# Strassen weight sums made by adding transfers from GpSimd

## The chip, the cores and the metric

One core of a Trainium2 chip runs the whole program in one launch. The metric is the device time of an execution in microseconds (us); the median of three runs is given. The engines are TensorE (PE; its weight loads are shown as PEld), VectorE (DVE), ScalarE (ACT), GpSimd (POOL) and SyncE (SP), which here issues nearly all loads. All work on SBUF, with matmul results in PSUM, and 16 DMA engines move data between device memory and SBUF.

## What is computed

A decoder trunk of two layers over 512 tokens with 16 meta tokens ahead of them, width 1024. Each layer is an FFN, a mixer (gated linear attention in the first layer, windowed attention in the second) and another FFN, each between two RMS norms:

```python
def swiglu(x, w_in, w_out):
    gate, up = jnp.split(x @ w_in, 2, axis=-1)
    return (jax.nn.silu(gate) * up) @ w_out

for layer in range(DEPTH):                      # DEPTH = 2, D_FF = 2816 = 22 tiles of 128
    g = norm_gains[layer]
    h = h + 0.5 * rmsnorm(swiglu(rmsnorm(h, g[0]), w_ffn_in[layer, 0], w_ffn_out[layer, 0]), g[1])
    hn = rmsnorm(h, g[2])
    mix = ...                                   # gla_mixer, or swa_mixer over shared k, v
    h = h + rmsnorm(mix, g[3])
    h = h + 0.5 * rmsnorm(swiglu(rmsnorm(h, g[4]), w_ffn_in[layer, 1], w_ffn_out[layer, 1]), g[5])
```

The four FFNs are where the change lies.

## The kernel before

All is in float32; a product is made of three fast matmuls, for which each operand is split in a high part and a rest. A weight tile comes from device memory into a *raw* tile of 128 x 512 (a pool of `RAWS` tiles, reused in turn). ScalarE copies it, rounded, into the first half of a `w` tile, and VectorE writes raw minus that copy into the second half: that is a *split*. Then TensorE may use the `w` tile, and the raw tile is free for a later load.

Each FFN goes over its 22 hidden tiles in chunks of 4, 6, 6 and 6. The first chunk is computed plainly. In each of the other three, a hidden tile needs a gate weight g and an up weight u, each 128 x 1024; they are taken together as a 2 x 2 block matrix with the blocks 11 and 12 (the halves of g) and 21 and 22 (the halves of u), and multiplied with the tokens by a Strassen scheme: seven products instead of eight, of twelve matmuls each. Their weight operands are 11, 12, 22 and the four sums

- s1 = 21 + 22, s3 = 11 + 21, s2 = s1 + 11, s4 = s2 + 12.

With four FFNs and 18 such hidden tiles in each there are 72 pairs, and twelve chunks of six pairs, which are called stages here. A stage ends with the output projection of its six hidden tiles (names `y` and `Y`).

The order of TensorE's instructions is written down while the program is built, by a small planner (class `Flow`): it advances a clock by the estimated time of each matmul, and coroutines that split, evacuate and prefetch are put in where their time has come. `load_unit` issues the loads of the next weight unit, `split_pair` (L251) splits the seven operands of a pair at steps of `STEP`, `slot` holds a split back until one of the `w` tiles may be taken, and `prefetch` asks for units up to a number of slots ahead, with at most `CHAINS` = 2 pairs unfinished. SP carries the loads, in order; a load waits only until the raw tile that it reuses has been split. `Strassen.head`, `body` and `tail` give the products in the order 11, then s4 and 22 of the pair before, then s1, s2, 12, s3. Between them ScalarE copies banks away (`d` at L909, `c` at L915 and L917) and VectorE sums (`c` at L922, L931, L937, L938), so that a bank can be used again.

In `split_pair`, the sums are made by VectorE in place in the four raw tiles (L266), between the splits. GpSimd makes square sums for the norms (L447) and roots; it issues no transfers.

Of the kernel before, what the change touches and what calls it, by code (L numbers as in the profile page):

```python
# [13 lines left out]
ALU = mybir.AluOpType  # L14
# [15 lines left out]
L1 = [(16, 256), (272, 256)]  # L30
L1W = [(16, 512)]
SLOTS = 32
RAWS = 8
RING = 10
STEP = 1.1
CHAINS = 2
# [103 lines left out]
def trunk_kernel(ctx: ExitStack, tc, a, out, last_out):  # L140
    nc = tc.nc
    pe, act, dve, pool, sp = nc.tensor, nc.scalar, nc.vector, nc.gpsimd, nc.sync
    flow = Flow()

    cp = ctx.enter_context(tc.tile_pool(name="cp", bufs=1))
    rp = ctx.enter_context(tc.tile_pool(name="rp", bufs=RAWS))
    hp = ctx.enter_context(tc.tile_pool(name="hp", bufs=SLOTS))
# [14 lines left out]
    def pair_tile(name, dt=F32R):  # L162
        return hp.tile([P, 2, TOK], dt, tag="pair", name=name)
# [54 lines left out]
    used, asked, freed, ahead, cap, dma_end = [0], [0], [0], [16], [len(units)], [0.0]  # L218
# [10 lines left out]
    def slot(i):  # L229

        while live[0] + sum(n for j, n in owed.items() if j < i) >= limit[0]:
            yield room[0]
        live[0] += 1
        owed[i] -= 1

    def raw_tile(name):
        return rp.tile([P, 512], F32, tag="raw", name=name)
# [7 lines left out]
    def split_unit(i, raws):  # L245
        yield 2.2
        for raw, m in raws:
            yield from slot(i)
            split_part(i, raw, m)

    def split_pair(i, raws):  # L251


        r11, r12, r21, r22 = raws
        parts, ready = loaded[i]

        def part(name, src):
            yield from slot(i)
            w = pair_tile(f"w{i}_{name}")
            act.activation(w[:, 0, :512], src, AF.Copy)  # L260
            dve.tensor_tensor(w[:, 1, :512], src, w[:, 0, :512].bitcast(F32), op=ALU.subtract)  # L261
            parts[name].append(w)
            ready[name].finish(flow)

        def add(dst, src):
            dve.tensor_tensor(dst, dst, src, op=ALU.add)  # L266

        yield 2.2
        yield from part("11", r11)
        add(r11, r21)  # L270
        add(r21, r22)
        yield STEP
        yield from part("s1", r21)
        yield STEP
        yield from part("s3", r11)
        add(r11, r22)
        yield STEP
        yield from part("s2", r11)
        yield STEP
        yield from part("12", r12)  # L280
        add(r12, r11)
        yield STEP
        yield from part("s4", r12)
        yield STEP
        yield from part("22", r22)
        chains[0] -= 1
        prefetch()

    def load_unit():
        i = len(loaded)  # L290
        asked[0] += costs[i]
        owed[i] = costs[i]
        if isinstance(units[i], list):
            g, u = units[i]
            chains[0] += 1
            raws = [raw_tile(f"raw{i}_{k}") for k in range(4)]
            for k in (2, 0, 1, 3):
                sp.dma_start(raws[k], (g, u)[k // 2][:, k % 2 * 512 : (k % 2 + 1) * 512])
                dma_end[0] = max(dma_end[0], flow.clock) + 512 * 1.5e-3
            names = ("11", "12", "22", "s1", "s2", "s3", "s4")  # L300
            loaded.append(({k: [] for k in names}, {k: Job(None) for k in names}))
            gen = split_pair(i, raws)
        else:
            n = units[i].shape[-1]
            raws = []
            for c in range(0, n, 512):
                m = min(512, n - c)
                raws.append((raw_tile(f"raw{i}_{c}"), m))
                sp.dma_start(raws[-1][0][:, :m], units[i][:, c : c + m])
            dma_end[0] = max(dma_end[0], flow.clock) + n * 1.5e-3  # L310
            loaded.append([])
            gen = split_unit(i, raws)
        split_jobs.append(flow.spawn(gen, dma_end[0] - flow.clock))

    def prefetch():
        while len(loaded) < cap[0] and asked[0] + costs[len(loaded)] <= freed[0] + ahead[0]:
            if isinstance(units[len(loaded)], list) and chains[0] == CHAINS:
                break
            load_unit()
# [1149 lines left out]
    raws = [[raw_tile(f"raw{i}_{c}") for c in (0, 512)] for i in range(2)]  # L1469
# [18 lines left out]
    x.rjob[0] = flow.spawn(factors(0, opened), SQUARES)  # L1488
    dma_end[0] = 1.0
    load_unit()  # L1490
    load_unit()
    load_h(1, 0, 2, 4, 6)
    flow.spawn(second(), SECOND)
# [134 lines left out]
```

## Time and profile before

| what | value |
|---|---|
| time, median of 3 runs | 1878.98 us (1878.68 to 1879.55) |
| span of the profiled execution | 1876.7 us |
| its distance to the median | 2.3 us; no separate time of the profiled execution is listed |
| instructions in the span | 37,247 |
| mean GB/s of all DMA | 93 |
| bytes through SP's queue | 171.74 MB |

The page gives busy times by engine, and the span in 40 slices; a group of instructions is listed by its line, engine, operation and tiles, with its count, total and mean time, and behind the bar the idle time of its engine just before it and what ended that idle time. A matmul's time there is longer than the step to the next one, since matmuls overlap. The chain of waits goes back from the last instruction, at each step to what released it.

### The profile page before, as it was taken

How to read it: one execution, taken by the hardware profiler on the slowest of the kernel's cores; microseconds unless marked ns; L12 is line 12 of the kernel's file. 1: busy time of each engine (PE TensorE's matmuls, PEld its weight loads, DVE VectorE, ACT ScalarE, POOL GpSimd, SP SyncE). 2: the span in 40 equal slices, each digit the busy share in tenths (PEclk: the TensorE clock that was granted, in tenths of full speed). 3: DMA queues.
4: the chain of work that ended last, by engine and by line, in shares of the span. 5: the costliest groups of instructions: out<-in, count | busy, mean ns of one | idle time of the engine just before them, and what ended most of it. 6: DMA issues, size and time to landing. Idle time of an engine off the chain costs nothing.

```text
span 1876.7 us, 37247 instructions
## 1 busy us (share of the span) xinstructions
PE 1866.2 (99%) x14463; PEld 1784.7 (95%) x14463; DVE 1395.9 (74%) x2837; ACT 1027.2 (55%) x2309; POOL 163.6 (9%) x295
## 2 busy tenths in 40 slices
PE   9999999999999999999999999999999999999998
PEld 9999999999999999999999898989988898989898
DVE  7885858767564788585887886868777679858585
ACT  5663535654446566363674553535767856636364
POOL 2000000330001300000033000000320140000002
PEclk9999999999999999999999999999999999999999
DMA  5333333421123123233351223233421212333331
GB/s 172 98 96 101 93 106 96 138 69 57 62 63 113 46 91 102 91 102 96 102 175 46 69 88 115 89 114 95 143 74 52 69 46 74 101 104 103 102 114 59
DMA packets 102273, 174.70 MB, mean 93 GB/s; under 512 B 11856, under 2 KB 24016, under 8 KB 102096
## 3 DMA queue, kind: packets, MB, share of 16 engines
q1 hardware_dynamic: 101664, 171.74, 29.3%
q8 instruction: 113, 1.85, 0.4%
q14 instruction: 64, 0.52, 0.1%
q10 hardware_dynamic: 432, 0.59, 0.1%
HBM read 169.66 MB, written 2.10 MB: 92 GB/s over the span
## 4 chain that ended last, share of the span: by engine, by line
PE 90%; DVE 7%; ACT 2%; issue 1%; DMA 0%; POOL 0%; DVEq 0%; SPq 0%; ACTq 0%; POOLq 0%
PE y L177 31%; PE a L177 19%; PE x L177 19%; PE c L177 8%; PE d L177 5%; PE o L177 1%; DVE raw L266 1%; ACT w_s L260 1%; DVE w_s L261 1%; PE e L177 1%; DVE w L261 1%; PE po L177 1%; DVE w L242 1%; PE sa L177 1%; PE pt L189 1%
## 5 line engine op out<-in xcount | busy, mean ns | idle before, releaser
L261 DVE TENSOR_TENSOR w_s<-raw,w_s 128x512 fp32r<-128x512 f32 x288 | 193.8, 690 | 130.1 <-ACT w_s L260 128.3
L177 PE MATMUL y<-hidl0f,w 128*128 128x256 f32 (+1 forms) x2112 | 262.4, 285 | 1.1 <-DVE hidl0f L453 0.9
L177 PEld LDWEIGHTS y<-hidl0f,w 128*128 128x128 f32 x2112 | 259.3, 188 | 2.2 <-DVE hidl0f L453 1.5
L242 DVE TENSOR_TENSOR w<-raw,w 128x512 fp32r<-128x512 f32 x376 | 235.4, 654 | 32.1 <-ACT w L241 30.3
L260 ACT ACTIVATE w_s<-raw 128x512 fp32r<-128x512 f32 x288 | 175.3, 628 | 150.8 <-DVE raw L266 137.6
L177 PE MATMUL y<-hidl1f,w 128*128 128x512 f32 (+1 forms) x1344 | 251.4, 346 | 0.8 <-DVE hidl1f L453 0.4
L177 PEld LDWEIGHTS y<-hidl1f,w 128*128 128x128 f32 x1344 | 212.2, 188 | 36.0 <-DVE hidl1f L942 1.6
L241 ACT ACTIVATE w<-raw 128x512 fp32r<-128x512 f32 x376 | 206.9, 586 | 41.9 <-PE y L177 29.9
L266 DVE TENSOR_TENSOR raw<-raw,raw 128x512 f32<-128x512 f32 x288 | 197.9, 687 | 5.5
L447 POOL TENSOR_TENSOR acc_post<-acc_post,sq_post 128x256 f32<-128x256 f32 (+1 forms) x77 | 62.6, 813 | 1534.0 <-ACT sq_post L446 1531.6
L261 DVE TENSOR_TENSOR w<-raw,w 128x512 fp32r<-128x512 f32 x216 | 148.3, 687 | 29.8 <-ACT w L260 29.0
L260 ACT ACTIVATE w<-raw 128x512 fp32r<-128x512 f32 x216 | 134.0, 621 | 41.6 <-PE y L177 41.0
L177 PE MATMUL x<-x_l0m,w 128*128 128x272 f32 (+1 forms) x1152 | 152.0, 288 | 0.0
L177 PEld LDWEIGHTS x<-x_l0m,w 128*128 128x128 f32 x1152 | 143.3, 188 | 2.7 <-issue 1.7
L706 DVE TENSOR_TENSOR Y<-y,Y 128x256 f32<-128x256 f32 (+2 forms) x175 | 81.8, 473 | 72.1 <-PE y L177 71.5
L177 PE MATMUL a<-zl0f_t,w_s 128*128 128x264 f32 x864 | 117.2, 285 | 0.0
L177 PE MATMUL a<-zl1f_t,w_s 128*128 128x256 f32 x864 | 114.7, 282 | 1.0 <-ACT c L917 0.5
L177 PEld LDWEIGHTS a<-zl1f_t,w_s 128*128 128x128 f32 x864 | 107.4, 188 | 3.0 <-ACT c L917 2.0
L177 PEld LDWEIGHTS a<-zl0f_t,w_s 128*128 128x128 f32 x864 | 109.9, 188 | 0.3
L177 PE MATMUL x<-x_l0f,w 128*128 128x256 f32 (+1 forms) x768 | 97.7, 287 | 1.2 <-ACT w L241 0.8
L177 PEld LDWEIGHTS x<-x_l0f,w 128*128 128x128 f32 x768 | 94.7, 188 | 2.2 <-ACT w L241 1.0
L177 PE MATMUL x<-x_l1f,w 128*128 128x256 f32 (+1 forms) x576 | 93.1, 320 | 0.5 <-ACT x_l1f L475 0.5
(513 smaller groups left out, 3216.6 us busy)
## 6 DMA issues: line engine op xcount, KB each, us to landing
raw<-in_w_in SPq DMA_DIRECT2D x352, 256.0 KB, 2.9
raw<-in_w_out SPq DMA_DIRECT2D x96, 256.0 KB, 3.2
raw<-in_w_last SPq DMA_DIRECT2D x48, 256.0 KB, 3.1
raw<-in_gla_in SPq DMA_DIRECT2D x48, 256.0 KB, 3.2
raw<-in_w_out SPq DMA_DIRECT2D x64, 128.0 KB, 2.9
raw<-in_gla_out SPq DMA_DIRECT2D x16, 256.0 KB, 2.8
raw<-in_w_q SPq DMA_DIRECT2D x16, 256.0 KB, 4.5
raw<-in_swa_out SPq DMA_DIRECT2D x16, 256.0 KB, 2.8
```

What stands on the lines that cost most here:

```text
L177: inst = pe.matmul(o, lhs, rhs, start=start, stop=stop, skip_group_check=onto)
L189: pe.transpose(o, src, ident)
L241: act.activation(w[:, 0, :m], raw[:, :m], AF.Copy)
L242: dve.tensor_tensor(w[:, 1, :m], raw[:, :m], w[:, 0, :m].bitcast(F32), op=ALU.subtract)
L260: act.activation(w[:, 0, :512], src, AF.Copy)
L261: dve.tensor_tensor(w[:, 1, :512], src, w[:, 0, :512].bitcast(F32), op=ALU.subtract)
L266: dve.tensor_tensor(dst, dst, src, op=ALU.add)
L447: pool.tensor_tensor(sums[0][:, :n], sums[0][:, :n], t[:, :n], op=ALU.add)
L706: dve.tensor_tensor(y, p[:, :n], y, op=ALU.add)
```

## The change

The four sums are no longer made by VectorE. Each pair now takes seven raw tiles: 11, 12 and 22 as before, and one tile for each sum. SP loads one addend of each sum into its tile by a plain transfer (21 into s1 and into s3, 11 into s2, 12 into s4). GpSimd then issues four transfers that add their source to what the tile holds: 22 from device memory to s1, 11 from device memory to s3, the finished s1 to s2, and the finished s2 to s4, the last two from SBUF to SBUF. The splits run in the order 11, s1, s2, 12, s3, s4, 22. The pool of raw tiles grows from 8 to 14, and the scratch space reserved in SBUF for such transfers goes from the default to 4096 bytes per partition. The planner's figure for the end of a pair's transfers counts 11 of them instead of 4.

```diff
-RAWS = 8
+RAWS = 14
...
-        r11, r12, r21, r22 = raws
+        r11, r12, r22, s1, s3, s2, s4 = raws
...
-        def add(dst, src):
-            dve.tensor_tensor(dst, dst, src, op=ALU.add)
-
         yield 2.2
         yield from part("11", r11)
-        add(r11, r21)
-        add(r21, r22)
         yield STEP
-        yield from part("s1", r21)
+        yield from part("s1", s1)
         yield STEP
-        yield from part("s3", r11)
-        add(r11, r22)
-        yield STEP
-        yield from part("s2", r11)
+        yield from part("s2", s2)
         yield STEP
         yield from part("12", r12)
-        add(r12, r11)
         yield STEP
-        yield from part("s4", r12)
+        yield from part("s3", s3)
+        yield STEP
+        yield from part("s4", s4)
         yield STEP
         yield from part("22", r22)
...
-            raws = [raw_tile(f"raw{i}_{k}") for k in range(4)]
-            for k in (2, 0, 1, 3):
-                sp.dma_start(raws[k], (g, u)[k // 2][:, k % 2 * 512 : (k % 2 + 1) * 512])
-                dma_end[0] = max(dma_end[0], flow.clock) + 512 * 1.5e-3
+            a11, a12, a21, a22 = (b[:, c : c + 512] for b in (g, u) for c in (0, 512))
+            r11, r12, r22, s1, s3, s2, s4 = raws = [raw_tile(f"raw{i}_{k}") for k in range(7)]
+            for r, src in ((s1, a21), (s3, a21), (s2, a11), (r11, a11), (s4, a12), (r12, a12), (r22, a22)):
+                sp.dma_start(r, src)
+            for r, src in ((s1, a22), (s3, a11), (s2, s1), (s4, s2)):
+                pool.dma_start(r, src, accum_op=ALU.add)
+            dma_end[0] = max(dma_end[0], flow.clock) + 11 * 512 * 1.5e-3
...
-    nc = bacc.Bacc("TRN2", target_bir_lowering=False, num_devices=1)
+    nc = bacc.Bacc("TRN2", target_bir_lowering=False, num_devices=1, dynamic_dma_scratch_size=4096)
```

## The prediction

> **What bounds the kernel now.** I read the page's shares first, then the chain that ended last, then the stages by windows, then who waits for whom, and last the single products of one stage.
>
> ```profile
> PE 1866.2 (99%) x14463; PEld 1784.7 (95%) x14463; DVE 1395.9 (74%) x2837; ACT 1027.2 (55%) x2309; POOL 163.6 (9%) x295
> ...
> PE 90%; DVE 7%; ACT 2%; issue 1%; DMA 0%; POOL 0%; DVEq 0%; SPq 0%; ACTq 0%; POOLq 0%
> ...
> L266 DVE TENSOR_TENSOR raw<-raw,raw 128x512 f32<-128x512 f32 x288 | 197.9, 687 | 5.5
> ```
>
> TensorE is busy for all but 10.5 us of the span of 1876.7 us. The third row is the work that the change takes away: 288 VectorE adds, four for each of 72 weight pairs, 687 ns each. They look like a large prize (197.9 us, and the chain goes through VectorE for 7%), so the question is whether TensorE ever waits for them. The Strassen stages answer it (one row per stage; columns are busy us and counts, then clock, DMA share and GB/s):
>
> ```profile
> 180.00:243.00 63.00, 63.00 (x519) 63.00 (x518) 50.17 (x92) 36.90 (x79) 0.00 (x0) 1.00 0.35 102
> 277.00:340.00 63.00, 63.00 (x516) 62.84 (x515) 51.05 (x91) 38.55 (x81) 0.00 (x0) 1.00 0.36 113
> 883.00:946.00 63.00, 63.00 (x517) 62.85 (x516) 50.94 (x91) 38.49 (x80) 0.00 (x0) 1.00 0.37 112
> 1585.00:1648.00 63.00, 62.12 (x507) 60.84 (x506) 54.70 (x99) 37.50 (x83) 0.00 (x0) 1.00 0.35 109
> ```
>
> In the first three TensorE (63.00 of 63.00) has no gap, with VectorE at 80%; the fourth, the first such stage of the last FFN, is the worst of the twelve and loses 0.9 us. TensorE's own waits say the same (the first rows; the longest five come to 3.7 us, and those that end on ACT's copies `c` and `d`, which may stand behind a wait for the adds, to 0.9):
>
> ```profile
> PE busy L1443 <- DVE eps L1495: 1.0, 1, 1.0
> PE y L177 <- DVE hidl0f L453: 0.9, 3, 0.3
> PE x L177 <- ACT w L241: 0.8, 1, 0.8
> PE a L177 <- ACT c L917: 0.5, 1, 0.5
> PE x L177 <- ACT x_l1f L475: 0.5, 1, 0.5
> PE a L177 <- ACT d L909: 0.4, 1, 0.4
> ```
>
> So TensorE sets the time, its clock is 1.00 in these stages, and its instructions stand in the same order in the built changed program (13,981 before and after, none moved). What the change can give is bounded by the gaps; what it can cost is not.
>
> **What is removed.** Four adds per pair, 4 x 0.687 = 2.75 us of VectorE out of the 10.27 us that a pair takes, and with them ACT's wait for them:
>
> ```profile
> ACT w_s L260 <- DVE raw L266: 137.6, 164, 2.7
> ```
>
> These 137.6 us are ACT idling off the chain: TensorE is gapless over the stages in which they lie. Worth on the path: the 0.9 us of waits above that end on ACT inside the stages, and part of the 0.9 us for `hidl0f` where the factors of the first pair are made beside the first splits. I take 1.5 us, between 0 and the 10.5 us that TensorE idles at all; it lies near the low end because most of those 10.5 us are at the start, the end and in the mixers, where no pair is split.
>
> **What is added: transfers.** Per pair, SP issues 7 plain loads in place of 4, and GpSimd 4 adding transfers.
>
> ```profile
> 5.00:20.00 15.00, 13.85 (x106) 13.14 (x105) 13.59 (x22) 13.89 (x35) 6.08 (x7) 1.00 1.05 375
> raw<-in_w_in SPq DMA_DIRECT2D x352, 256.0 KB, 2.9
> L298 SPq DMA_DIRECT2D raw<-in_w_in x288: 327/328/1541, 56.0 to 1806.4; - x144
> DMA to landing us min/median/max: 2.2/3.0/6.6
> ```
>
> The first row is the opening, the one stretch where the 16 DMA engines are full (share 1.05): 375 GB/s, so 262,144 bytes take 0.70 us of all engines. Seven loads are 4.9 us. An adding transfer has to bring in both its source and its destination; its engine time is bounded by 0.70 us (one pass) and, if reads set the pace, 1.40 us (two passes). I take 1.40, since both operands pass: 4.9 + 5.6 = 10.5 us per pair, against 10.27 us of TensorE; by one pass it would be 7.7. [...] Full engines are still not a full stage: a stage of six pairs and its output projection repeats every 97 us (first two rows of the stages), and needs 6 x 10.5 + 8 x 1.5 x 0.70 = 71 us of DMA, 74%. SP's issuing is 7 x 0.328 = 2.3 us per pair, hidden in SP's own waits for free raw tiles.
>
> **What is added: waits in a row on GpSimd.** The built order on its queue is, for each pair, s1, s3, s2, s4. s2 adds the finished s1 to its tile, s4 adds the finished s2, and the next pair's s1 stands behind s4. Call L the time from GpSimd's start on an adding transfer to its landing, and i its own time for one. In steady state GpSimd needs per pair: L (s1 lands), L (s2 lands), i (s4 sent): P = 2L + i. For i the nearest row is a GpSimd instruction on a tile of similar size:
>
> ```profile
> L447 POOL TENSOR_TENSOR acc_post<-acc_post,sq_post 128x256 f32<-128x256 f32 (+1 forms) x77 | 62.6, 813 | 1534.0 <-ACT sq_post L446 1531.6
> ```
>
> I take i = 0.8 us. L is a plain landing (3.0 median) + a second pass (0.70) + i = 4.5 us; its bounds are 2.2 (the fastest plain landing) and 13.2 (two of the slowest, 6.6). So P = 2 x 4.5 + 0.8 = 9.8 us, under 10.27: GpSimd keeps up, by 0.5 us. [...]
>
> **How late may a sum be?** One pair in products of 12 matmuls (start, length):
>
> ```profile
> 197.05 1.62 PE L177 MATMUL a<-zl0f,w 128*128 128x264 f32 x12
> 198.50 1.62 PE L177 MATMUL c<-zl0f,w_s 128*128 128x264 f32 x12
> 199.96 1.64 PE L177 MATMUL a<-zl0f_t,w 128*128 128x264 f32 x12
> 201.43 1.64 PE L177 MATMUL c<-zl0f_t,w_s 128*128 128x264 f32 x12
> 202.91 1.63 PE L177 MATMUL a<-zl0f_t,w_s 128*128 128x264 f32 x12
> 204.38 1.64 PE L177 MATMUL d<-zl0f,w 128*128 128x264 f32 x12
> 205.85 1.63 PE L177 MATMUL a<-zl0f_t,w_s 128*128 128x264 f32 x12
> 207.32 1.61 PE L177 MATMUL a<-zl0f,w 128*128 128x264 f32 x12
> ...
> 197.95 0.42 DVE L922 TENSOR_TENSOR c<-a,c 128x264 f32<-128x264 f32 x1
> 204.58 0.39 ACT L917 ACTIVATE c<-a 128x264 f32<-128x264 f32 x1
> ...
> L261 DVE TENSOR_TENSOR w_s<-raw,w_s 128x512 fp32r<-128x512 f32 x288 | 193.8, 690 | 130.1 <-ACT w_s L260 128.3
> L260 ACT ACTIVATE w_s<-raw 128x512 fp32r<-128x512 f32 x288 | 175.3, 628 | 150.8 <-DVE raw L266 137.6
> ```
>
> The first eight are 11 of pair m, s4 and 22 of m-1, then s1, s2, 12, s3 of m, and 11 of m+1: a pair every 10.27 us, a product every 1.47; below them stand the sum `v` (0.42), a copy of a bank (0.39) and the two halves of a split (0.69 and 0.63). Put t = 0 at the end of s1 (202.9). In the changed order, s3 of pair m is split just before t = 0, which frees its raw tile, and then SP sends s3, s2 and the rest for pair m+2, since 14 raw tiles are two pairs. They land at 3.3; GpSimd sends s3 and then s2 at about 4.3, and s2 lands at 4.3 + L = 8.8. ACT comes to the split of that s2 after the copy of s2 of m+1, at 11.75 + 0.4 + 0.6 = 12.7. Behind it on ACT stand the copies for the next products, and on VectorE the sum `v` that must be out of bank `a` before 22 of m+1 starts at 17.6; with 0.7 + 0.7 + 0.4 us of VectorE and 0.6 of ACT in between, ACT may start that split as late as 15.2 with no harm. Slack: 15.2 - 4.3 - L = 10.9 - L, here 6.4 us. At the start of a stage the splits of its first pair run early, under the output projection, so the first three pairs' sums are there, and only the last three of six live on the chain. The chain hurts where two steps of drift eat the slack: 2 (2L + 0.8 - 10.27) = 10.9 - L, at L = 6.0. I forecast L = 4.5 and so a cost of nothing; the cover is 6.4 us.
>
> **What moves.** VectorE's and ACT's splits change places with the factor parts at the four FFN starts and with a few gains at the ends; the gaps credited above lie there, and I count nothing more. At a stage's end the sixth output weight's second half reuses the raw tile of the last 22, five ACT instructions earlier; it lands some 3 us after that split (3.0 above), while the next instruction that TensorE needs from ACT, the SiLU after the last s4, is due three products (4.4 us) and one piece of projection (1.9, below) after. Covered, with 2 us to spare; uncovered it costs some 1 us at each of 12 places.
>
> ```profile
> 236.62 2.04 PE L177 MATMUL y<-hidl0f,w 128*128 128x272 f32 x15
> 238.50 1.61 PE L177 MATMUL a<-zl0f_t,w_s 128*128 128x264 f32 x12
> ```
>
> SBUF: six more raw tiles of 2 KB per partition are the 12 KB that the smaller scratch gives back. GpSimd's square sums and roots stand behind all adding transfers of their FFN, which are over by then.
>
> **Sum.** 1878.98 (median of the runs; the profiled span of 1876.7 lies 2.3 below it, and the sum is made on the span: 1876.7 - 1.5 + 0 = 1875.2, plus 2.3) gives 1877.5 us.
>
> **Rivals.** 0.2% (3.8 us) is about what a measurement of this kernel can tell from no change.
>
> (a) The GpSimd chain becomes the bound: slower. Past L = 6.0 a stage loses 5 (L - 6.0), and there are 12: 60 us for each us of L. With the slowest plain landing, 6.6 + 0.7 + 0.8 = 8.1, it is 126 us; at L = 7.0, 60 us, so 1938. For it: the DMA engines would be nearly full while pairs are read, and the full opening is where landings were slow; nothing here shows an adding transfer. Against: a spare 1.5 us. Chance 0.27.
>
> (b) An adding transfer costs the engines far more than two passes. At four passes (2.8 us) a pair needs 4.9 + 11.2 = 16.1 us and a stage 6 x 16.1 + 8.4 = 105 us of the 97: at least 12 x 8 = 96 us, 1974. By two passes it decides nothing. Chance 0.13.
>
> (c) Small losses at the borders: L a little over 6 in some stages, or the stage ends uncovered by 1 us each: 5 to 15 us, 1884 to 1894. Chance 0.12.
>
> (d) More of TensorE's idle time goes than I credit: over 3.8 of 10.5 us. Against it: only 1.8 us of waits lead back to a splitting engine near the pairs. Chance 0.05.
>
> That the change doesn't do what it says is excluded by the built order: 288 VectorE instructions fewer, 288 GpSimd transfers more.
>
> **Numbers.** The forecast within 0.2% has 0.43, and is the likeliest single case; slower is 0.27 + 0.13 + 0.12 = 0.52; faster 0.05. The range runs from 1873 (the gap credit at its largest likely value, 6 us) to 1985, which takes in (b) at four passes and (a) up to L of 7.8 and leaves out under 2 in 10. The likeliest case's own range is 1875 to 1882.
>
> **What would show it.** The adding transfers should land in about 4.5 us, GpSimd should idle between pairs, the DMA share in the stages rise from 0.35 to 0.8 to 1.0, `ACT w_s <- DVE raw` vanish, and TensorE stay at 63.00 of 63.00. ACT waiting for a DMA at L260 with gaps on TensorE in the fourth to sixth pair of a stage would prove (a); gaps with DMA share at 1.0 throughout and loads of output weights late too, (b).

## The result, and the profile after

The changed kernel takes 1908.66 us (median of 4 runs, 1903.59 to 1917.42), the kernel before 1878.99 us beside it: a ratio of 1.0162, interval [1.0149, 1.0175]. It is 29.7 us slower. The profiled execution has a span of 1907.0 us against 1876.7.

From the page of the changed kernel: busy time of each engine, the DMA engines' busy tenths in 40 slices, and the two queues that carry loads (q1, SP's) and adding transfers (q0, GpSimd's), with packets, MB and share of the 16 engines' span.

```profile
PE 1874.6 (98%) x14463; PEld 1790.3 (94%) x14463; DVE 1219.2 (64%) x2549; ACT 1008.7 (53%) x2309; POOL 417.3 (22%) x583
...
DMA  6788879421123268888952588989421226888881
...
q1 hardware_dynamic: 132768, 228.37, 36.6%
q0 software_dynamic: 41472, 75.52, 24.3%
```

VectorE lost 176.7 us of busy time (1395.9 to 1219.2; its adds had taken 197.9), and still the time rose. TensorE has the same 14463 instructions in the same order. Its idle time rose from 10.5 us to 1907.0 - 1874.6 = 32.4, by 21.9; its busy time rose by 8.4. Together that is the 30.3 us of the span. Both parts have their place in the rows: first who waits for whom (total, times, longest), then two of the stages by window.

```profile
PE a L177 <- DVE c L918: 13.1, 12, 5.5
PE a L177 <- ACT d L905: 7.8, 7, 2.6
PE a L177 <- ACT c L913: 1.3, 4, 0.5
...
ACT w_s L260 <- DMA raw<-raw: 77.4, 26, 7.1
```

```profile
180.00:243.00 63.00, 62.37 (x509) 61.94 (x509) 37.73 (x69) 33.97 (x76) 12.29 (x14) 1.00 0.83 200
277.00:340.00 63.00, 61.10 (x495) 60.89 (x494) 35.32 (x64) 31.45 (x69) 13.67 (x16) 0.99 0.88 209
```

The wait of ACT's splits for VectorE's sums (137.6 us) is gone. In its place ACT waits at L260 for an adding transfer to land: only 26 times, but for up to 7.1 us. TensorE's three waits above (22.2 us in all, against 0.9 before) are for copies and sums that free the banks; in the two stalls followed below, these stand on ACT and VectorE behind such a split. The DMA share of a stage rose from 0.35 to 0.83 and 0.88.

One stall, as the timelines show it (start, length, then the idle time before an instruction and what ended it). GpSimd, from the fifth pair's last sum to the sixth's, in the first stage:

```profile
121.47 0.87 POOL L294 DMA_DIRECT2D raw<-raw  x1 [5.01 <-issue]
122.01 2.12 POOL L294 DMA_DIRECT2D raw<-in_w_in  x2
129.38 0.87 POOL L294 DMA_DIRECT2D raw<-raw  x1 [5.25 <-DMA raw<-in_w_out]
136.83 0.87 POOL L294 DMA_DIRECT2D raw<-raw  x1 [6.58 <-issue]
```

These are s4 of one pair, then s1 and s3, s2, and s4 of the next. s2 stands 7.37 us behind s1 and s4 7.45 us behind s2, though GpSimd itself works for under 1 us on each. From s4 to s4 it takes 15.4 us; TensorE uses up a pair in 10.27. ACT and TensorE at the same place:

```profile
130.30 0.41 ACT L241 ACTIVATE w<-raw 128x256 fp32r<-128x256 f32 x1
136.17 0.63 ACT L260 ACTIVATE w_s<-raw 128x512 fp32r<-128x512 f32 x1 [5.46 <-DMA raw<-raw]
...
138.06 0.37 ACT L905 ACTIVATE d<-a 128x264 f32<-128x264 f32 x1
```

```profile
135.42 1.62 PE L177 MATMUL c<-zl0f_t,w_s 128*128 128x264 f32 x12
138.48 1.74 PE L177 MATMUL a<-zl0f_t,w_s 128*128 128x264 f32 x12 [1.44 <-ACT d L905]
```

ACT has come to the split of s2, waits 5.46 us for its landing, and the copy of bank `d` that TensorE needs stands behind it and three more splits: it comes at 138.06, and TensorE has stood still for 1.44 us. This is the sixth pair of the stage, on which drift has had time to add up. The longest stall, 5.46 us from 1834, has the same form: ACT comes to a split of s2 at 1836.87 after 7.08 us of waiting, and the sum on VectorE that TensorE needs stands behind that split, at 1838.93.

The 8.4 us of longer busy time are mostly the clock. Windows again (PE's busy time is the first figure behind the comma, the granted clock the third from the end), around a stall of 1.90 us at 335, behind the longest one, of 5.46 us, at 1834, and around one of 2.61 us at 1333:

```profile
337.00:338.40 1.40, 1.40 (x12) 1.40 (x13) 0.91 (x3) 0.43 (x1) 0.00 (x0) 1.00 0.77 181
338.40:341.80 3.40, 3.40 (x17) 3.40 (x16) 2.68 (x6) 2.63 (x6) 0.00 (x0) 0.50 0.44 96
...
1836.80:1843.60 6.80, 4.20 (x19) 4.20 (x20) 3.01 (x7) 2.88 (x7) 2.66 (x3) 0.50 0.78 141
...
1332.00:1342.00 10.00, 7.39 (x51) 7.19 (x50) 7.33 (x14) 7.29 (x16) 0.87 (x1) 0.83 0.56 160
```

Three times while TensorE has work the granted clock is halved, for 3.4 us, for 6.8 us, and, by the 0.83 of the last row, for 10 x 0.17 / 0.5 = 3.4 us. TensorE is busy for 3.4, 4.2 and 3.2 us of these (the third from 1335.08 to 1338.49), and half of that, 5.4 us, is lost; the rest is part of the stalls. So of the 30 us some 22 are stalls and 5 their echo in the clock; the last 3 were not traced.

### The profile page after: what moved, and what is told of

The parts are those of the page before. It is cut to its first block, busy times and chain, and to the rows that moved or that the text cites. A ratio compares the mean times of both kernels' runs of the same rounds, so it can differ in the third digit from the quotient of the medians.

```text
span 1907.0 us, 38387 instructions
## 1 busy us (share of the span) xinstructions
PE 1874.6 (98%) x14463; PEld 1790.3 (94%) x14463; DVE 1219.2 (64%) x2549; ACT 1008.7 (53%) x2309; POOL 417.3 (22%) x583
## 5 line engine op out<-in xcount | busy, mean ns | idle before, releaser
L294 POOL DMA_DIRECT2D raw<-raw x144 | 125.6, 872 | 695.7 <-DMA raw<-in_w_in 194.6
L242 DVE TENSOR_TENSOR w<-raw,w 128x512 fp32r<-128x512 f32 x376 | 233.9, 654 | 27.1 <-ACT w L241 25.5
L260 ACT ACTIVATE w_s<-raw 128x512 fp32r<-128x512 f32 x288 | 176.8, 625 | 116.8 <-DMA raw<-raw 77.4
L241 ACT ACTIVATE w<-raw 128x512 fp32r<-128x512 f32 x376 | 207.2, 586 | 36.7 <-PE y L177 25.5
L294 POOL DMA_DIRECT2D raw<-in_w_in x144 | 141.2, 1175 | 253.9 <-DMA raw<-in_w_in 108.3
L261 DVE TENSOR_TENSOR w<-raw,w 128x512 fp32r<-128x512 f32 x216 | 144.0, 688 | 69.1 <-ACT w L260 67.6
L260 ACT ACTIVATE w<-raw 128x512 fp32r<-128x512 f32 x216 | 129.3, 624 | 24.3 <-PE y L177 23.0
L905 ACT ACTIVATE d<-a 128x264 f32<-128x264 f32 (+1 forms) x72 | 26.8, 372 | 176.5 <-PE a L177 176.3
```

The lines of the kernel that those rows point to most:

```text
L241: act.activation(w[:, 0, :m], raw[:, :m], AF.Copy)
L242: dve.tensor_tensor(w[:, 1, :m], raw[:, :m], w[:, 0, :m].bitcast(F32), op=ALU.subtract)
L294: pool.dma_start(r, src, accum_op=ALU.add)
L905: act.activation(self.d, t.a, AF.Copy)
```

## The experiments

Every time is given against runs of the kernel before on the same chip, with the interval of the ratio. A *pass* is the engine time of one plain 256 KB load, 0.80 us by q1's row above; an adding transfer took 1.61 us by q0's, two passes, so that the changed kernel, with 7 loads and 4 adding transfers per pair, has 15. The *chain* is s1, s2, s4, each of which waits on GpSimd's queue for the one before to land. One thing more can differ between versions: the planner's figure for the end of a pair's transfers. It is 11 in the changed kernel and in the six runs that change its adding transfers alone (chain broken, another order, 16 columns, 256 columns, s3 plain, s3 third); in the traces of all seven, ACT and VectorE have the same instructions in the same order. The versions with three sums, two (one link too) and one have 9, 7 and 6 there, and the kernel before 4, which moves their splits among the other instructions of ACT and VectorE.

**The chain or the bytes.** The first run keeps every transfer and breaks the chain: s2 and s4 add a block that is there already.

```diff
-for r, src in ((s1, a22), (s3, a11), (s2, s1), (s4, s2)):
+for r, src in ((s1, a22), (s3, a11), (s2, r11), (s4, r11)):
```

> The changed kernel, but the third and fourth adding transfer of a pair take the tile of block 11 as their source (SBUF to SBUF, same size) in place of s1 and s2, so that no adding transfer waits for another; s2 and s4 are left wrong. Same bytes, same number of transfers, same order on every queue. Theory A (the chain of adding transfers on GpSimd's queue, 2 landings per pair, is the bound): the stages return to 63 of 63 us of TensorE and the time to 1878 to 1884. Theory B (the 16 DMA engines are full, whatever the order): 1900 to 1915, with the same DMA share of 0.8 to 0.9 in the stages.

Measured: 1876.89 us against 1878.67, ratio [0.9981, 1.0000]. One stage of it:

```profile
180.00:243.00 63.00, 63.00 (x518) 63.00 (x517) 40.86 (x76) 36.23 (x81) 12.20 (x15) 1.00 0.84 220
```

At the same DMA share (0.84 against 0.83) TensorE has no gap in this stage, and over the run the adding transfers take as long to land (median, last figure) as in the changed kernel, whose rows stand further below:

```profile
raw<-in_w_in POOLq DMA_DIRECT2D x144, 256.0 KB, 6.3
raw<-raw POOLq DMA_DIRECT2D x144, 256.0 KB, 6.0
```

A DMA share of 0.84 and landings of 6.3 and 6.0 us alone cost nothing here; theory B, as it stood, is out. The time is even 1.1 us under theory A's range.

**Another order.** s4's transfer is sent behind the next pair's s1, so that a landing of one pair runs beside one of the next.

```diff
...
-for r, src in ((s1, a22), (s3, a11), (s2, s1), (s4, s2)):
-    pool.dma_start(r, src, accum_op=ALU.add)
+first = pool.dma_start(s1, a22, accum_op=ALU.add)
+last_sum(first)          # s4 of the pair before, behind first
+pool.dma_start(s3, a11, accum_op=ALU.add)
+pool.dma_start(s2, s1, accum_op=ALU.add)
+pending.append((s4, s2))
...
```

The helper `last_sum` sends what is pending; it is also called ahead of the split of s4.

> The changed kernel with one exchange on GpSimd's queue per pair: the fourth adding transfer (s4) of a pair is issued behind the first (s1) of the next pair instead of ahead of it, so that the next s1 lands while s2 does. All sums stay right; every transfer and all other queues are as in the changed kernel. Theory A: the steady period on GpSimd falls from two landings (some 13 to 15 us per pair) to one landing plus four issues (6.6 + 3.8 = 10.4 us or less), so the drift goes: 1878 to 1888. Theory B: no change, 1900 to 1915.

Measured: 1883.07 us, ratio [1.0014, 1.0033]: 25 of the 30 us are back with all bytes, all sums and all waits kept. What hurts is the waits standing in a row.

**Two sums, no chain.** s1 and s3, which depend on no other sum, stay adding transfers; s2 and s4 go back to VectorE. Five loads, 9 passes, 10 raw tiles.

```diff
-r11, r12, r22, s1, s3, s2, s4 = raws
+r11, r12, r22, s1, s3 = raws
...
+        add(r11, s1)             # s2, by VectorE
...
+        add(r12, r11)            # s4
...
```

> Only s1 and s3 are made by adding transfers, s2 and s4 by VectorE in place as before; 5 raw tiles per pair, 10 kept, scratch of 4096. No adding transfer waits for another, and a pair needs 5 + 2 x 2 = 9 passes of 0.70 us = 6.3 us of the DMA engines instead of 10.5. Both theories: 1876 to 1881, as the chain is gone and the engines have room; if even two adding transfers hurt, above 1885.

Measured: 1874.71 us (1874.42 to 1875.41), ratio [0.9969, 0.9988]. That is 4.0 us under the kernel before, and 1.3 us under the range expected.

**Raw tiles alone**: the kernel before with `RAWS = 14` and the small scratch.

```diff
-RAWS = 8
+RAWS = 14
...
-    nc = bacc.Bacc("TRN2", target_bir_lowering=False, num_devices=1)
+    nc = bacc.Bacc("TRN2", target_bir_lowering=False, num_devices=1, dynamic_dma_scratch_size=4096)
```

> The kernel before with the 14 raw tiles and the scratch of 4096 alone, all sums on VectorE. Both theories: within 0.1% of before, 1877 to 1881; a third theory (the larger pool lets loads run ahead and collide) would give over 1885.

Measured: 1878.77 us against 1878.67, ratio [0.9991, 1.0010]. Nothing.

**Three sums, the chain kept.** s3 is made by VectorE from s2; s1, s2 and s4 are as in the change. Six loads, 12 passes.

```diff
-RAWS = 14
+RAWS = 12
...
+        dve.tensor_tensor(r11, s2, r22, op=ALU.subtract)   # s3, behind the split of s2
...
-for r, src in ((s1, a22), (s3, a11), (s2, s1), (s4, s2)):
+for r, src in ((s1, a22), (s2, s1), (s4, s2)):
```

> The chain s1, s2, s4 stays on GpSimd's queue, two landings per pair; s3 alone is made by VectorE (s2 - 22, into block 11's tile). 6 loads and 3 adding transfers, 12 passes of 0.70 us = 8.4 us of the engines per pair in place of 10.5. Theory A (the two landings in a row are the bound, whatever the engines have spare): only GpSimd's 1.2 us for s3 and a little of the landing time go, so the period is 11 to 12.5 us against 10.27 and a good part of the loss stays: 1882 to 1895 us. Theory B (the engines' bytes set it): with 8.4 of 10.27 us the loss is gone, 1875 to 1877 us.

Measured: 1875.01 us against 1878.59, ratio [0.9972, 0.9990]. Theory A, that the chain is the bound whatever the engines have spare, is out as well. GpSimd in the same stage (s4, then s1, s2 and s4 of the next pair), and the transfers' time from issue to landing:

```profile
105.98 0.86 POOL L295 DMA_DIRECT2D raw<-raw  x1 [5.09 <-DVE c L934]
106.84 0.90 POOL L295 DMA_DIRECT2D raw<-in_w_in  x1
113.34 0.86 POOL L295 DMA_DIRECT2D raw<-raw  x1 [5.61 <-ACT d L906]
119.08 0.86 POOL L295 DMA_DIRECT2D raw<-raw  x1 [4.87 <-DVE w_s L261]
```
```profile
raw<-in_w_in SPq DMA_DIRECT2D x496, 256.0 KB, 3.9
raw<-raw POOLq DMA_DIRECT2D x144, 256.0 KB, 4.4
```

s2 comes 6.50 us behind s1 and s4 5.74 us behind s2, where the changed kernel has 7.37 and 7.45; from s4 to s4 it is 13.1 us in place of 15.4. That is still more than 10.27, and yet nothing is lost; that the lead of the first pairs of a stage covers the difference is the prediction's picture, and was not shown by itself. The changed kernel's transfers, for comparison:

```profile
raw<-in_w_in SPq DMA_DIRECT2D x568, 256.0 KB, 5.1
raw<-in_w_in POOLq DMA_DIRECT2D x144, 256.0 KB, 6.6
raw<-raw POOLq DMA_DIRECT2D x144, 256.0 KB, 5.0
```

So a theory C took the place of both, and is tested below: the loss is the chain times the landing, and the landing is long where the pair's own bytes fill the engines. Three more runs went with this one. First the version with two sums and 14 tiles:

```diff
-RAWS = 10
+RAWS = 14
```

> The version with s1 and s3 by adding transfers, with 14 raw tiles in place of 10. If that version's gain needs no more tiles than two pairs, 1874 to 1876 us as with 10. If the loads were still waiting for tiles somewhere on the path, up to 1 us less.

Measured: 1875.56 us, ratio [0.9974, 0.9992], as with 10.

One link: s1 and s2 by adding transfers, the rest by VectorE, 9 passes.

```diff
+        dve.tensor_tensor(r11, s2, r22, op=ALU.subtract)   # s3
...
+        dve.tensor_tensor(r12, r12, s2, op=ALU.add)        # s4
...
-for r, src in ((s1, a22), (s3, a11), (s2, s1), (s4, s2)):
+for r, src in ((s1, a22), (s2, s1)):
```

> s1 and s2 by adding transfers, s3 (as s2 - 22) and s4 by VectorE: as many loads, adding transfers and raw tiles as the version with s1 and s3 (1874.7 us), but s2's transfer waits for s1's to land. Theory A: only one landing per pair holds the queue, so the period is about 5.5 + 0.9 = 6.4 us, well under 10.27, and nothing is lost: 1874 to 1877 us. If any chain of adding transfers costs TensorE time, 1880 us or more.

Measured: 1874.80 us, ratio [0.9970, 0.9989]. A single landing to wait for costs nothing here.

One sum, s1, and three by VectorE in place. This edit is against the kernel before, and keeps that kernel's order of splits (s3 before s2):

```diff
-        add(r11, r21)
-        add(r21, r22)
+        add(r21, r11)            # s3, ahead of
+        add(r11, s1)             # s2
...
-        add(r11, r22)
...
+            pool.dma_start(s1, a22, accum_op=ALU.add)
...
```

> Only s1 is an adding transfer (5 loads, 1 add, 7 passes = 4.9 us of the engines per pair); s2, s3 and s4 are VectorE's. No transfer waits for another. If the gain comes from the VectorE time that is taken away, it should be about half of that of the version with two sums (4 us): 1876 to 1878 us. If it comes from the place of the first adds at the border of an FFN alone, it is there in full: 1874 to 1876.

Measured: 1880.81 us, ratio [1.0002, 1.0021], 2.2 us slower than before, though it takes work off VectorE and has no chain. Both expectations missed. Its trace has one wait that neither the kernel before nor the version with two sums shows:

```profile
DVE raw L266 <- DMA raw<-in_w_in: 41.5, 32, 3.5
```

VectorE's first sum stands at the head of its queue until a plain load has landed. Whether that is the cause, or the order of splits, in which it differs from the other versions, was not tried.

**The bytes as a dose.** s3's transfer in the changed kernel is cut in width; GpSimd's queue, its order and its waits stay.

```diff
-for r, src in ((s1, a22), (s3, a11), (s2, s1), (s4, s2)):
+for r, src in ((s1, a22), (s3[:, :16], a11[:, :16]), (s2, s1), (s4, s2)):
```

> The changed kernel with s3's adding transfer cut to 16 of its 512 columns (s3 is left wrong): GpSimd's queue holds the same four transfers in the same order with the same waits, and the engines carry some 13 passes of 0.70 us = 9.1 us per pair in place of 10.5. Theory A as first stated (the two landings in a row on GpSimd's queue are the bound whatever the engines have spare): the loss stays, 1895 to 1910 us. Theory C (the landings in the chain are only long because the pair's own transfers fill the engines, 10.5 of 10.27 us): the landing of s2's and s4's transfers falls below 5 us, the period from 14.9 to 13 us or less as in the version with three sums, and the time to 1875 to 1882 us.

> The same with s3's adding transfer cut to 256 of 512 columns: 14 passes, 9.8 of 10.27 us of the engines per pair. Theory A: 1895 to 1910 us. Theory C: between the small version and the changed kernel, 1878 to 1895 us.

Measured: 1892.39 us with 16 columns, ratio [1.0060, 1.0090], and 1900.99 us with 256, ratio [1.0082, 1.0149]. The loss falls with the bytes, from 29.7 us to 22.3 and 13.7, which theory A as first stated does not have; but theory C missed both times as well. The run with 16 columns lies under theory A's range and far over theory C's (1875 to 1882), and the one with 256 lies inside theory A's (1895 to 1910) and over theory C's (1878 to 1895). Two runs asked whether the rest is s3's turn on GpSimd's queue: one without that transfer, so that s3's tile keeps block 21, and one that keeps it but puts s2 ahead of it.

```diff
-for r, src in ((s1, a22), (s3, a11), (s2, s1), (s4, s2)):
+for r, src in ((s1, a22), (s2, s1), (s4, s2)):
```

```diff
+second = pool.dma_start(s2, s1, accum_op=ALU.add)
+after(second, pool.dma_start(s3, a11, accum_op=ALU.add))
```

> The changed kernel without s3's adding transfer (its tile keeps block 21 alone, so s3 is left wrong): 7 loads and 3 adding transfers, 13 passes = 9.1 us of the engines per pair, as in the version that cut s3's transfer to 16 columns (1892.4 us), but one transfer less on GpSimd's queue; s1, s2 and s4 follow on each other as before. Theory C (bytes fill the engines and stretch the chain's landings): as that version, 1888 to 1895 us. Theory D (what a short fourth transfer still costs is its turn on GpSimd's queue between s1 and s2): as the version with three sums, 1875 to 1879 us.

> The changed kernel with GpSimd's order s1, s2, s3, s4 in place of s1, s3, s2, s4: all bytes, all waits, the same sums; s3's transfer no longer stands between s1 and s2 but runs while s2's lands. Theory C: the same bytes in the same time and two landings in a row, so the period and the time stay within a few us of the changed kernel's, 1900 to 1912 us. Theory D: s3's turn of 0.5 to 1.2 us leaves the chain, 1885 to 1895 us.

Measured: 1890.92 us, ratio [1.0037, 1.0083], and 1910.24 us, ratio [1.0147, 1.0181]. Both lie in theory C's ranges, which had been set with the 1892 us known: the turn on the queue is worth little.

**One load more.** Left open was why three sums with 12 passes lose nothing and three with 13 lose 12 us. The version with three sums got a seventh raw tile per pair, filled by a load that VectorE then writes over.

```diff
+        dve.tensor_tensor(s3, s2, r22, op=ALU.subtract)
...
-for r, src in ((s1, a22), (s3, a11), (s2, s1), (s4, s2)):
+for r, src in ((s1, a22), (s2, s1), (s4, s2)):
```

> The version with three sums (s3 made by VectorE as s2 - 22; 1875.0 us) with a seventh raw tile per pair that SP fills with block 21 before VectorE writes s3 over it: the same sums and the same three adding transfers, and one load per pair (13 passes, 9.1 us, in place of 12, 8.4) and two kept tiles more. Theory C (bytes beside the chain stretch its landings): as the version whose s3 is a plain load, 1885 to 1894 us. Theory E (it is not the bytes; the version with three sums is quick because its s3 does not come from a raw tile of its own): 1875 to 1878 us.

and, for the tiles alone, the version with three sums with `RAWS = 14`:

> The version with three sums with 14 raw tiles kept in place of 12 and nothing else: 6 loads and 3 adding transfers per pair as before. Theory C and E: 1874 to 1877 us. If tiles kept ahead were what hurts (loads sent earlier, in a burst that meets the chain), 1880 us or more.

Measured, the tiles alone: 1876.43 us, ratio [0.9977, 0.9996]. With the load: 2040.07 us, ratio [1.0835, 1.0871], which neither theory has. The edit had done something else: with a tile of its own, s3's sum was no longer tied to the splits, and was put ahead of the previous pair's on VectorE. The wait of that sum, in all and once on VectorE's timeline:

```profile
DVE raw L271 <- DMA raw<-raw: 224.7, 45, 7.3
```
```profile
117.94 0.69 DVE L271 TENSOR_TENSOR raw<-raw,raw 128x512 f32<-128x512 f32 x1 [6.47 <-DMA raw<-raw]
118.55 0.43 DVE L928 TENSOR_TENSOR c<-c,c 128x264 f32<-128x264 f32 x1
```

The sums of banks (`c`) stand behind a VectorE instruction that waits 6.47 us for s2's landing. The run was made again with that sum pinned behind the split of s2, where the version with three sums has it.

```diff
+        after(half[0], dve.tensor_tensor(s3, s2, r22, op=ALU.subtract))   # half[0]: s2's second half
```

> The version with the seventh raw tile filled, with VectorE's sum for s3 held behind the second half of s2's split, where the version with three sums has it: in the run before, that sum had moved ahead of the previous pair's splits on VectorE and waited there for s2's landing (VectorE waited 224.7 us in all for adding transfers), which cost 161 us and hid the question. Now the sums, transfers and their order are those of the version with three sums, with one load per pair (13 passes in place of 12) and two kept tiles more. Theory C (the bytes beside the chain stretch its landings): 1885 to 1894 us, as the version whose s3 is a plain load (1890.9 us). Theory E (not the bytes): 1875 to 1878 us, as the one with 14 tiles and no load more (1876.4 us).

Measured: 1889.40 us against 1878.68, ratio [1.0039, 1.0072]. With one load of 256 KB more per pair and two kept tiles, a gain of 3.6 us becomes a loss of 10.7; the tiles alone do not do that. But the edit, made from the changed kernel, also has its 11 as the planner's figure in place of 9, which starts a pair's splits 2 x 512 x 1.5e-3 = 1.5 us later in the plan: in the two traces ACT's and VectorE's instructions stand in another order in some 60 and 80 places, while with the tiles alone they stand as they were. So the load and the new order were not tried apart.

All together, by passes per pair, with the time against the kernel before:

| passes | chain s1, s2, s4 broken or eased | chain whole |
|---|---|---|
| 7 | +2.2 (one sum) | |
| 9 | -4.0 (two sums), -3.0 (the same, 14 tiles), -3.8 (one link) | |
| 12 | | -3.6 (12 tiles), -2.7 (14 tiles) |
| 13 | | +10.7 (load added), +12.4 (s3 plain), +13.7 (16 columns) |
| 14 | | +22.3 (256 columns) |
| 15 | -1.8 (chain broken), +4.4 (s4 sent later) | +29.7 (the change), +31.7 (s3 third) |

The planner's figure is 11 in the rows of 13 to 15 passes, so that the step from 13 to 15, and the chain broken at 15, are free of it; the step from 12 to 13 is not.

ACT's wait for a chained landing falls with the loss, if not in every step; the change has 77.4 us in 26 waits. Its row in the other runs with the chain whole, from s3 third, 256 columns, 16 columns, s3 plain, the load added, and 12 passes with 12 tiles:

```profile
ACT w_s L260 <- DMA raw<-raw: 64.8, 24, 6.5
```
```profile
ACT w_s L260 <- DMA raw<-raw: 56.9, 21, 7.1
```
```profile
ACT w_s L260 <- DMA raw<-raw: 41.6, 20, 5.7
```
```profile
ACT w_s L260 <- DMA raw<-raw: 32.2, 16, 5.4
```
```profile
ACT w_s L261 <- DMA raw<-raw: 38.0, 15, 5.4
```
```profile
ACT w_s L260 <- DMA raw<-raw: 2.0, 3, 0.8
```

The starts on GpSimd in these traces show what the bytes do. From s1 to s4, two links, it takes in the median of the 72 pairs 11.4 and 11.5 us in the two traces of 12 passes, 12.3 to 12.4 in the three of 13, 12.9 with 14 and 13.1 in the change (12.2 in s3 third, where s3 no longer stands between s1 and s2). So more bytes do make a longer chain. They do not give the size of the loss: from s4 to s4, over the last three pairs of each stage, the median is 13.2 and 13.6 us with 12 passes but 15.1 to 16.0 us in all six traces with more, while their losses go from 10.7 to 31.7 us. That part stays open.

## Why the prediction was wrong, point by point

The forecast was 1877.5 us, 1.5 us faster than before; the kernel came out 29.7 us slower, inside the outer range (1873 to 1985) but on the side of rival (a).

**The step that failed** is the third, the GpSimd chain: "L is a plain landing (3.0 median) + a second pass (0.70) + i = 4.5 us", and from it "GpSimd keeps up, by 0.5 us". The form was right: 2 x 7.4 + 0.5 (s4 at 121.47, s1 at 122.01) is the 15.4 us measured for the sixth pair. A link was 7.4 us in place of 4.5. Some 6.8 us of it are L as it was defined (GpSimd starts on s2 at 129.38, ACT's split of it starts at 136.17), and 0.7 us pass from that landing to GpSimd's next start, a term that the sum did not have. L had been made from a landing in stages with a DMA share of 0.35, while the step before it had already put 10.5 us of transfers into each 10.27 us of a pair. In engines that full the plain loads themselves took 5.1 us in place of 2.9, and L rose with them. The trace before had this landing: the loads of its opening, from 5 to 20 us, which gave the 0.70 us of a pass, took

```profile
DMA to landing us min/median/max: 5.0/5.6/6.6
```

and 5.6 + 0.70 + 0.8 = 7.1 us would have been past the threshold of 6.0. Rival (a) names these slow landings; the sum did not use them. The two steps were worked out apart, and so were the rivals: (b), full engines, was to decide nothing at two passes. It does decide, by way of (a).

**The threshold** L = 6.0 was near. With three sums a link is (6.50 + 5.74) / 2 = 6.1 us in the pair shown and nothing is lost; with the change it is 7.4 and a lot is. **The price** of 60 us per us of L was too high: at 7.4 it gives 84 us, and 30 were lost. The loss is uneven: by the starts of the stages' first products in the two traces, the last stages of the four FFNs, each with what follows it, carry 23 of the 30 us, and the other eight 7, between -1.0 and 2.8 each. Where the formula has its excess was not separated.

**Rival (a)** is what happened, with the signs that it named: gaps late in a stage (at the sixth pair, in the last stage at the fifth), and ACT waiting for a DMA at L260. It had 0.27. Its two worked cases were dearer than what came, 60 us at L = 7.0 and 126 at 8.1.

**The engines' price** of an adding transfer was right: 0.243 x 1907.0 / 288 = 1.61 us of all 16 engines, by q0's row. A plain 256 KB by q1's row is 0.366 x 1907.0 x 0.262 / 228.4 = 0.80 us. That is two passes. Rival (b)'s four passes are out. The pass itself is 0.80 us and not the 0.70 of the opening, so a pair needs 7 x 0.80 + 4 x 1.61 = 12.0 us of the engines, more than TensorE's 10.27; a stage still has room, as the run without the chain shows.

**TensorE's order and what the adds are worth.** That VectorE's adds were hardly on the path was right: with the chain broken the change is worth 1.8 us, near the credit of 1.5, though the interval of that run reaches up to no change. (The traces hold TensorE's 14463 matmuls in one order; the prediction's count of 13,981 stands in none of them.) The versions with fewer adding transfers gained up to 4.0 us, with another order on ACT and VectorE, so this is not the worth of the adds alone. The bound used, TensorE's idle time, misses some of it; of the version with three sums:

```profile
PE 1863.8 (99%) x14463; PEld 1784.4 (95%) x14463; DVE 1258.0 (67%) x2621; ACT 1011.1 (54%) x2309; POOL 352.2 (19%) x511
```
```profile
1585.00:1648.00 63.00, 63.00 (x511) 61.91 (x510) 42.28 (x80) 35.27 (x80) 10.48 (x12) 1.00 0.78 201
```

TensorE's idle time is 1873.4 - 1863.8 = 9.6 us, 0.9 less than before, and its busy time 2.4 us less, for the same matmuls; that short waits had been counted as busy would explain it, and was not shown. The stage at 1585, the worst of the kernel before with 62.12, has no gap.

**The stage ends**, called covered with 2 us to spare, gave no loss with the chain broken. **The tiles and the scratch** cost nothing, as counted. The echo in the clock, 5.4 us, was in no step.

## What to carry to other kernels

Here waits on transfers that themselves wait for transfers cost landings, 6.8 us in the link followed above, and not bandwidth (29.7 us were lost with the chain, none without it at a DMA share of 0.84), and the landings were those of the load that the change made, not of the one before it (5.1 us for a plain load, against 2.9): work out the engines' share first and take the landing from a stretch of the trace that has that share. Moving adds into transfers paid here, by 2 to 4 us, in the versions with two sums, with one link and with three sums in a row at 12 passes, where the DMA share of the stage at 180 was 0.56, 0.58 and 0.74; one sum alone did not pay, for a reason that was not found. At 13 to 15 passes the whole chain lost 10.7 to 31.7 us, and with s4 sent later, at 15, 4.4: where the engines are as full as that, leave the dependent sums to an engine that is off the path, or put other work between them on the queue. And when two versions differ by one unit, see that the planner has not moved anything else: here the step from 12 to 13 passes came with a new order on two engines.

## What the runs showed of the hardware that was not expected

In the changed kernel the clock fell after a stall of 1.90 us. TensorE around the drop at 338.4:

```profile
333.36 1.62 PE L177 MATMUL c<-zl0f_t,w_s 128*128 128x264 f32 x12
336.88 1.80 PE L177 MATMUL a<-zl0f_t,w_s 128*128 128x264 f32 x12 [1.90 <-ACT d L905]
338.48 2.84 PE L177 MATMUL d<-zl0f,w 128*128 128x264 f32 x12
```

It had been idle for 1.90 us, worked at full clock for another 1.5, and only then ran at half clock for 3.4 us (a product of 12 matmuls took 2.84 us in place of 1.62). The stall of 1.44 us at 137 has no such echo (clock 1.00):

```profile
133.80:146.00 12.20, 10.49 (x83) 10.06 (x82) 7.95 (x16) 7.97 (x19) 0.87 (x1) 1.00 0.49 132
```

By the clock records of this trace the drops start whole multiples of 3.413 us apart (338.39, 1335.08 and 1836.84) and last 3.413, 3.413 and 6.827 us. The 3.41 us ahead of each of the three, and a fourth stretch at such a multiple:

```profile
334.97:338.39 3.42, 1.52 (x13) 1.51 (x13) 2.87 (x6) 2.28 (x6) 0.87 (x1) 1.00 0.76 213
1331.67:1335.08 3.41, 1.05 (x9) 0.84 (x8) 1.60 (x3) 2.27 (x5) 0.87 (x1) 1.00 0.33 121
1833.42:1836.84 3.42, 0.52 (x5) 0.32 (x3) 0.00 (x0) 0.00 (x0) 0.00 (x0) 1.00 0.71 184
956.20:959.61 3.41, 1.73 (x15) 1.52 (x13) 3.41 (x8) 2.42 (x5) 0.00 (x0) 1.00 0.93 297
```

TensorE was idle for 1.90, 2.36 and 2.90 us in the three (its ends are modelled). In the fourth it was idle for 1.68 us, and no drop follows: the stall there, of 1.82 us up to 959.76, lies in it and, for its end, in the next. Leaving out the start and the end, no other such stretch of this trace at full clock has as much; the next has 1.44 us, from 137.00. What follows an idle time between 1.68 and 1.90 us the trace does not show.

GpSimd spends 0.87 us on an adding transfer from SBUF in the median (0.86 to 1.11 in the changed kernel). In the version with 16 columns it spends 0.87 us on s1's 512 columns, at 91.93, and 0.87 us on s3's 16, at 93.59; two sent together take 2.12 us at 122.01 in the changed kernel. What its queue loses is the waiting between them: the 288 instructions take 266.8 us (125.6 + 141.2), and GpSimd is idle for 949.6 (695.7 + 253.9) just before them.
